# Weight buffers 64 bytes apart, a later pair of column sums, and four raw buffers in a hybrid decoder layer

## The chip, the core and the metric

The kernel runs on one core of one Trainium2 chip. The metric is device time in microseconds of one execution. TensorE multiplies, ScalarE (ACT) and VectorE (DVE) prepare operands and do the element-wise work, GpSimd (POOL) does a few powers and issues some stores, SyncE (SP) issues the loads.

## The reference, cut to what matters

One layer, 256 tokens, width 2048, all in float32:

```
h     = RMSNorm(x)
proj  = h @ W_in        # 2048 x 8192: h_conv, b, c, z_conv, q, k, v, z_attn, 1024 columns each
conv  = b * causal_depthwise_conv_w3(c * h_conv)
attn  = attention(QKnorm(q), QKnorm(k), v)       # 8 heads of 128, causal, one block of 256
y     = concat[RMSNorm(conv) * silu(z_conv), RMSNorm(attn) * silu(z_attn)]
out   = x + y @ W_out   # 2048 x 2048
```

## The kernel before

**Precision.** Every float32 weight and activation is split into a high and a low part of type fp32r, and a product is made as high times high, high times low and low times high. The weights arrive as `raw`; ACT copies the high part into `wh` (L465) and DVE subtracts it into `wl` (L466).

**Pieces.** The work is a list of 160 pieces of 512 KB of weights (L427 to L432), in this order:

- 48 pieces of the token projections q, k, v ("A"): the weight tile is the moving operand, 512 columns, and a 128 x 128 slice of the input `xs` is stationary. Three matmuls (L106 to L108) for each k-tile and each half of the tokens, so 12 matmuls in a piece.
- 80 pieces of the channel projections ("B", `by_chan`): here the weight slice is stationary and the input moves. There are 20 units of four pieces: the four groups of z_attn first, then h, c, b and z_conv for each of four channel groups. For each of four k-tiles and two 128-channel blocks of a piece there is a pair: L473 moves 512 columns (high and low input) past `wh`, L474 moves 256 columns (high input) past `wl`. Eight pairs in a piece, 640 in all.
- 32 pieces of the output projection ("Y"), again three matmuls of 512 columns.

**Buffers.** `raw`, `wh` and `wl` have five buffers each (L52), 4096 bytes a partition. The constants in front are padded (L64, L314), and in the built program every `wh`, `wl` and `xs` slice that TensorE reads begins at a multiple of 512 bytes. The constant `ones` begins 64 bytes behind such a multiple of 128.

**Order.** The order is written out by hand. At piece j the program issues the load of piece j + 6 and the split of piece j + 3, then the matmuls of piece j, then what the table `todo` holds for this slot (`at(slot, f)`). A load waits on SP until DVE has read the buffer's former content; the queue of SP is in order, so the loads behind it wait too.

**Sums over channels.** The two output norms need a sum of squares over channels. `add_squares` adds up squares on ACT and DVE; `token_sums(slot, key, f)` then, at `slot`, splits the sum into `row_h` and `row_l` (ACT L129, DVE L130), two slots later multiplies both by `ones` on TensorE (L136, L137: 256 columns each), and one slot later takes the diagonal on DVE (L144) and the root on POOL (L111). For the attention ("a") the slot is `A_DONE + 4` = 70: the two matmuls stand behind piece 72, the 25th of the 80 channel pieces. For the convolution ("c") they stand behind the first output piece. What the sums are needed for, `gather` (L485), begins with the end of the first output unit.

Of the kernel before, what the change touches and what calls it, by code (L numbers as in the profile page):

```python
# [10 lines left out]
F32 = mybir.dt.float32  # L11
FR = mybir.dt.float32r
# [5 lines left out]
P = 128  # L18
# [3 lines left out]
KT = DM // P  # L22
DG = 1024
CW = 512
# [17 lines left out]
LEAD = 3  # L42
LOADS = LEAD + 3
SINGLE = 4
NWARM = 8


@with_exitstack
def hybrid_layer(ctx: ExitStack, tc: tile.TileContext, xT, x, w_a, w_b, w_out, par, out):
    nc = tc.nc  # L50
    cst = ctx.enter_context(tc.tile_pool(name="cst", bufs=1))
    wp = ctx.enter_context(tc.tile_pool(name="wp", bufs=LEAD + 2))  # L52
# [7 lines left out]
    def aux():  # L60
        return ps.tile([P, CW], F32, name="aux", bufs=4)
# [12 lines left out]
    a = aux()  # L74
    for i in range(NWARM):
        nc.tensor.matmul(a, warm[:, :P], warm, start=i == 0, stop=i == NWARM - 1)
    spark = cst.tile([P, 1], F32, name="spark")
# [17 lines left out]
    def at(slot, f, *args):  # L95
        todo.setdefault(slot, []).append((f, args))
# [19 lines left out]
    def add_squares(key, src):  # L116

        sq = tp.tile([P, CW], F32, name="sq", bufs=2)
        nc.scalar.activation(sq, src, AF.Square)
        if key not in sums:  # L120
            s = sums[key] = cst.tile([P, SEQ], F32, name="sums_" + key)
            nc.vector.tensor_add(s, sq[:, :SEQ], sq[:, SEQ:])
        else:
            for i in range(2):
                nc.vector.tensor_add(sums[key], sums[key], sq[:, i * SEQ:(i + 1) * SEQ])

    def split_rows(src):
        hi, lo = (tp.tile([P, SEQ], FR, name=n, bufs=1) for n in ("row_h", "row_l"))
        nc.scalar.activation(hi, src, AF.Copy)  # L129
        nc.vector.tensor_tensor(lo, src, hi.bitcast(F32), op=OP.subtract)  # L130
        return hi, lo

    def partition_sums(hi, lo):

        a = aux()
        nc.tensor.matmul(a[:, :SEQ], ones, hi, start=True, stop=False)  # L136
        nc.tensor.matmul(a[:, :SEQ], ones, lo, start=False, stop=True)  # L137
        return a

    def by_token(dst, a):  # L140

        for t in range(NT):
            d = tp.tile([P, P], F32, name="diag", bufs=2)
            nc.vector.tensor_tensor_reduce(out=d, in0=a[:, t * P:(t + 1) * P], in1=ident, scale=1.0, scalar=0.0,  # L144
                                           op0=OP.mult, op1=OP.add, accum_out=dst[:, t:t + 1])

    def token_sums(slot, key, f):

        def summed(a):
            ms = tp.tile([P, NT], F32, name="ms_t", bufs=2)  # L150
            by_token(ms, a)
            f(ms)

        at(slot, lambda: at(slot + 2, lambda hl=split_rows(sums[key]): at(slot + 3, summed, partition_sums(*hl))))
# [4 lines left out]
    def load_xT(k, n):  # L159
        if k % 2 == 0:  # L160
            x_raw[k // 2] = t2k((P, 2, SEQ))
        nc.sync.dma_start(x_raw[k // 2][:, k % 2:k % 2 + n], xT[:, k:k + n])  # L162
        if k == 0:
            nc.sync.dma_start(prm, par)

    def split_x(k):
        src, g = x_raw[k // 2][:, k % 2], prm[:, G_IN + k:G_IN + k + 1]
        nc.scalar.activation(xs[:, k, 0], src, AF.Copy, scale=g)  # L168
        nc.vector.scalar_tensor_tensor(xs[:, k, 1], src, g, xs[:, k, 0].bitcast(F32), op0=OP.mult, op1=OP.subtract)
# [259 lines left out]
    pieces = []  # L429
    for kind, n, w, kts in units:  # L430
        pk, cols = (4, GW) if kind == "B" else (2, CW)
        pieces += [(kind, n, w[:, k:k + pk], k, k + pk == kts, pk, cols) for k in range(0, kts, pk)]  # L432
    raws, ws = {}, {}

    def load(j):
        if j >= len(pieces):
            return
        _, _, src, _, _, pk, cols = pieces[j]
        raw = raws[j] = wp.tile([P, pk, cols], F32, name="raw")
        if j < SINGLE:  # L440
            for i in range(2):
                nc.sync.dma_start(raw[:, i:i + 1], src[:, i:i + 1])  # L442
                load_xT(2 * j + i, 1)
            return
        if j < KT // 2:
            load_xT(2 * j, 2)
        nc.sync.dma_start(raw, src)

    def split(j):
        if j >= len(pieces):  # L450
            return
        raw = raws.pop(j)
        wh = wp.tile(list(raw.shape), FR, name="wh")
        wl = wp.tile(list(raw.shape), FR, name="wl")
        ws[j] = (wh, wl)
        if j < SINGLE:
            for i in range(2):
                nc.scalar.activation(wh[:, i], raw[:, i], AF.Copy)
                nc.vector.tensor_tensor(wl[:, i], raw[:, i], wh[:, i].bitcast(F32), op=OP.subtract)
                split_x(2 * j + i)  # L460
            return
        if j < KT // 2:
            for i in range(2):
                split_x(2 * j + i)
        nc.scalar.activation(wh, raw, AF.Copy)  # L465
        nc.vector.tensor_tensor(wl, raw, wh.bitcast(F32), op=OP.subtract)  # L466
# [34 lines left out]
    A_DONE = max(ends["A", len(A_ORDER) - 1] + 18, ends["B", NG - 1] + 3)  # L501
    for g in range(NG):
        at(ends["A", len(A_ORDER) - 1] + 12 + 2 * g, lambda g=g: add_squares("a", oT[:, g * GPT:(g + 1) * GPT]))
    token_sums(A_DONE + 4, "a", a_rms)
    e = ends["B", len(B_ORDER) - 2]
    token_sums(e + 3, "c", c_rms)
    at(e + 7, c_rms2)

    for j in range(LOADS):
        load(j)  # L510
    for j in range(LEAD):
        split(j)
    acc = None
    for j, (kind, n, _, k, last, pk, _) in enumerate(pieces):
        load(j + LOADS)
        split(j + LEAD)
        if k == 0:
            acc = ps.tile([P, 2, CW], F32, name="acc", bufs=2)
# [14 lines left out]
        else:  # L533
            n, k0 = n
# [62 lines left out]
```

## Time and profile before

| what | value |
|---|---|
| median of three runs | 472.22 us (471.61 to 472.26) |
| profiled execution | 470.43 us |
| its span, first to last instruction | 468.7 us |
| PE busy | 462.6 us, 99% |
| DVE busy / ACT busy / POOL busy | 303.9 / 242.6 / 20.1 us |
| DMA moved | 90.63 MB, mean 193 GB/s |
| granted TensorE clock | 0.999 of full speed |

How to read it: PE is busy almost from end to end, so the span is the sum of the times from the start of one matmul to the start of the next. Matmuls overlap in a pipeline: the duration that the profile gives for one is longer than the time to the next one's start, here by about 0.16 us for each. So rates are best read from the first and the last start of a group and its count, and the durations then tell by their differences which matmuls of a stretch come sooner or later.

### The profile page before, as it was taken

The page shows a single profiled execution, that of the slowest core. Times are in us where ns is not written, and L with a number is a line of the kernel's source. Part 1 is how long each engine was busy: PE and PEld are TensorE (multiplying, and loading weights), DVE is VectorE, ACT ScalarE, POOL GpSimd, SP SyncE. Part 2 cuts the span into 40 slices and gives each one's busy share as a digit, 9 for nine tenths or more (in the row PEclk, how much of TensorE's full clock was granted, in tenths as well). Part 3 has the DMA queues.
Part 4 walks back from the last instruction along what each step waited for, and adds up shares of the span by engine and source line. Part 5 has one row for each costly group of instructions (what it writes and reads, how often), then busy time and mean ns, then how long its engine had stood idle before and what let it go on. Part 6 is the DMA issues. An engine that isn't in the chain of part 4 may idle for free.

```text
span 468.7 us, 6428 instructions
## 1 busy us (share of the span) xinstructions
PE 462.6 (99%) x2416; PEld 394.6 (84%) x2416; DVE 303.9 (65%) x440; ACT 242.6 (52%) x337; POOL 20.1 (4%) x23
## 2 busy tenths in 40 slices
PE   8999999999999999999999999999999999999996
PEld 5788888888888888888888888888888888888885
DVE  5988767567475666678866675666666676566541
ACT  6975546465536667656545544455544553343320
POOL 1002200002020000000100000000000010000100
PEclk9999999999999999999999999999999999999999
DMA  8987664645665555555565556656655778766611
GB/s 256 392 258 244 206 211 140 191 136 170 180 196 162 181 172 153 166 187 179 185 206 184 188 180 190 202 185 187 199 191 175 219 238 259 246 187 201 219 67 47
DMA packets 27583, 90.63 MB, mean 193 GB/s; under 512 B 3232, under 2 KB 4512, under 8 KB 27552
## 3 DMA queue, kind: packets, MB, share of 16 engines
q1 hardware_dynamic: 27072, 88.65, 59.9%
q0 software_dynamic: 480, 1.57, 1.0%
q8 instruction: 19, 0.31, 0.3%
q14 instruction: 12, 0.10, 0.1%
HBM read 88.11 MB, written 2.10 MB: 192 GB/s over the span
## 4 chain that ended last, share of the span: by engine, by line
PE 95%; DMA 2%; SPq 1%; DVE 0%; ACT 0%; issue 0%
PE acc L473 31%; PE acc L474 16%; PE acc L107 14%; PE acc L108 14%; PE acc L106 14%; PE aux L107 1%; PE aux L106 1%; PE aux L108 1%; DMA raw<-in_w_a_dram 1%; DMA t2k<-in_xT_dram 1%; PE aux L223 1%; PE aux L283 1%; SPq L442 0%; PE aux L252 0%; PE aux L299 0%; SPq L162 0%
## 5 line engine op out<-in xcount | busy, mean ns | idle before, releaser
L466 DVE TENSOR_TENSOR wl<-raw,wh 128x1024 fp32r<-128x1024 f32 x156 | 190.3, 1223 | 99.5 <-ACT wh L465 99.1
L473 PE MATMUL acc<-xs,wh 128*128 128x512 f32 x640 | 223.4, 393 | 0.0
L465 ACT ACTIVATE wh<-raw 128x1024 fp32r<-128x1024 f32 x156 | 164.6, 1057 | 111.4 <-PE acc L108 59.5
L474 PE MATMUL acc<-xs,wl 128*128 128x256 f32 x640 | 179.1, 280 | 0.0
L473 PEld LDWEIGHTS acc<-xs,wh 128*128 128x128 f32 x640 | 119.9, 187 | 26.9
L474 PEld LDWEIGHTS acc<-xs,wl 128*128 128x128 f32 x640 | 120.9, 189 | 0.0
L106 PE MATMUL acc<-wh,xs 128*128 128x512 f32 x192 | 76.3, 397 | 0.4 <-ACT xs L168 0.4
L107 PE MATMUL acc<-wl,xs 128*128 128x512 f32 x192 | 75.1, 391 | 0.4 <-DVE wl L466 0.4
L108 PE MATMUL acc<-wh,xs 128*128 128x512 f32 x192 | 75.1, 391 | 0.0
L107 PE MATMUL acc<-wl,yh 128*128 128x512 f32 x112 | 43.6, 389 | 0.0
L108 PE MATMUL acc<-wh,yl 128*128 128x512 f32 x112 | 43.6, 389 | 0.0
L106 PE MATMUL acc<-wh,yh 128*128 128x512 f32 x112 | 43.6, 389 | 0.0
L106 PEld LDWEIGHTS acc<-wh,xs 128*128 128x128 f32 x192 | 36.3, 189 | 8.3 <-ACT xs L168 1.3
L107 PEld LDWEIGHTS acc<-wl,xs 128*128 128x128 f32 x192 | 36.4, 189 | 7.8 <-DVE wl L466 0.8
L108 PEld LDWEIGHTS acc<-wh,xs 128*128 128x128 f32 x192 | 36.2, 188 | 7.7
L338 ACT ACTIVATE t2k<-acc 128x512 f32<-128x512 f32 x20 | 11.9, 596 | 28.5 <-PE acc L474 28.5
L339 DVE TENSOR_TENSOR t2k<-acc,t2k 128x512 f32<-128x512 f32 x20 | 13.8, 691 | 18.1 <-ACT t2k L338 18.1
L106 PEld LDWEIGHTS acc<-wh,yh 128*128 128x128 f32 x112 | 21.0, 188 | 4.4
L108 PEld LDWEIGHTS acc<-wh,yl 128*128 128x128 f32 x112 | 21.0, 188 | 4.3
L107 PEld LDWEIGHTS acc<-wl,yh 128*128 128x128 f32 x112 | 21.0, 188 | 4.3
L308 ACT ACTIVATE yh<-t2k,prm 128x256 fp32r<-128x256 f32 x16 | 7.3, 503 | 16.6 <-DVE t2k L374 16.6
L111 POOL TENSOR_TENSOR r<-ms,neg_half 128x8 f32<-128x8 f32 x4 | 10.1, 2525 | 78.6 <-DVE ms L210 78.6
(117 smaller groups left out, 289.3 us busy)
## 6 DMA issues: line engine op xcount, KB each, us to landing
raw<-in_w_b_dram SPq DMA_DIRECT2D x80, 512.0 KB, 4.6
raw<-in_w_a_dram SPq DMA_DIRECT2D x44, 512.0 KB, 3.9
raw<-in_w_out_dram SPq DMA_DIRECT2D x32, 512.0 KB, 3.8
raw<-in_w_a_dram SPq DMA_DIRECT2D x8, 256.0 KB, 4.1
t2k<-in_x_dram SPq DMA_DIRECT2D x8, 256.0 KB, 4.8
out_dram<-t2k POOLq DMA_DIRECT2D x6, 256.0 KB, 3.4
t2k<-in_xT_dram SPq DMA_DIRECT2D x8, 128.0 KB, 4.1
t2k<-in_xT_dram SPq DMA_DIRECT2D x4, 256.0 KB, 5.6
```

What stands on the lines that cost most here:

```text
L106: nc.tensor.matmul(acc, sh, mh, start=first, stop=False)
L107: nc.tensor.matmul(acc, sh, ml, start=False, stop=False)
L108: nc.tensor.matmul(acc, sl, mh, start=False, stop=last)
L111: nc.gpsimd.tensor_tensor(dst, ms, neg_half[:, :ms.shape[-1]], op=OP.pow)
L223: nc.tensor.transpose(a[:, i * P:(i + 1) * P], qn[key, t][:, i], ident)
L308: nc.scalar.activation(yh[:, kt + i], src, AF.Copy, scale=g)
L338: nc.scalar.activation(d, acc[:, :, SEQ:], AF.Copy)
L339: nc.vector.tensor_add(d, acc[:, :, :SEQ], d)
L465: nc.scalar.activation(wh, raw, AF.Copy)
L466: nc.vector.tensor_tensor(wl, raw, wh.bitcast(F32), op=OP.subtract)
L473: nc.tensor.matmul(acc[:, b], wh, xs[:, k].rearrange("p s t -> p (s t)"), start=first, stop=False)
L474: nc.tensor.matmul(acc[:, b, :SEQ], wl, xs[:, k, 0], start=False, stop=last)
```

## The change

Three things are changed. The tiles `wh` and `wl` are allocated 64 floats wider (4352 bytes instead of 4096), and from piece `(n, k) >= (4, 8)` of the channel projections on (the third piece of the fifth unit, the 19th of the 80), `wh` is used from float 16 on, that is 64 bytes further; `wl` and all other pieces stay at the tile's start. To make room, `raw` has four buffers instead of five. And `token_sums` of the attention moves from slot `A_DONE + 4` to slot `e`, the last piece but four of the channel projections.

```
+SHIFT, SHIFT_FROM = 16, (4, KT // 2)
...
-        raw = raws[j] = wp.tile([P, pk, cols], F32, name="raw")
+        raw = raws[j] = wp.tile([P, pk, cols], F32, name="raw", bufs=LEAD + 1)
...
-        wh = wp.tile(list(raw.shape), FR, name="wh")
-        wl = wp.tile(list(raw.shape), FR, name="wl")
+        kind, n, _, k, _, pk, _ = pieces[j]
+
+        shift = SHIFT if kind == "B" and (n, k) >= SHIFT_FROM else 0
+        wh, wl = (wp.tile([P, 2 * CW + 64], FR, name=m)[:, o:o + 2 * CW].rearrange("p (k c) -> p k c", k=pk)
+                  for m, o in (("wh", shift), ("wl", 0)))
...
-    token_sums(A_DONE + 4, "a", a_rms)
     e = ends["B", len(B_ORDER) - 2]
+    token_sums(e, "a", a_rms)
     token_sums(e + 3, "c", c_rms)
```

In the built program the buffers of `wh` and `wl` stood 4096 bytes apart; now they stand 4352 bytes apart, so that they begin at multiples of 256 bytes and some of them no longer at multiples of 512. The lines of the changed file are five higher than before in the matmuls (L478 is L473, L479 is L474) and two higher in the sums (L138 is L136).

On TensorE, behind the 25th channel piece, before (the numbers tell the buffers apart):

```order
L474 MATMUL acc_2147<-xs_70,wl_2068 128x256
L136 MATMUL aux_2169<-row_h_2110,ones_89 128x256
L137 MATMUL aux_2169<-row_l_2111,ones_89 128x256
L473 MATMUL acc_2147<-xs_70,wh_2090 128x512
L474 MATMUL acc_2147<-xs_70,wl_2091 128x256
```

In the same place now:

```order
L478 MATMUL acc_2143<-xs_70,wh_2067 128x512
L479 MATMUL acc_2143<-xs_70,wl_2068 128x256
L478 MATMUL acc_2143<-xs_70,wh_2090 128x512
L479 MATMUL acc_2143<-xs_70,wl_2091 128x256
L478 MATMUL acc_2143<-xs_70,wh_2090 128x512
```

And two pieces ahead of the end of the channel projections, where only pairs stood before, now:

```order
L478 MATMUL acc_3419<-xs_70,wh_3367 128x512
L479 MATMUL acc_3419<-xs_70,wl_3368 128x256
L138 MATMUL aux_3466<-row_h_3409,ones_89 128x256
L139 MATMUL aux_3466<-row_l_3410,ones_89 128x256
L478 MATMUL acc_3419<-xs_70,wh_3389 128x512
L479 MATMUL acc_3419<-xs_70,wl_3390 128x256
```

The two matmuls with `ones` have moved 55 - 2 = 53 pieces back; from the last attention head to that place the stream is now pairs alone.

On SP, at the first load that is one whole piece (the fifth piece), before:

```order
L162 DMA t2k_137<-in_xT_dram 128x512 [waits DMAHW1_49]
L447 DMA raw_136<-in_w_a_dram 128x1024 [waits DMAHW2_49]
L162 DMA t2k_141<-in_xT_dram 128x512 [waits DMAHW3_49]
L447 DMA raw_140<-in_w_a_dram 128x1024 [waits DMAHW4_49,DVE_49]
L162 DMA t2k_175<-in_xT_dram 128x512 [waits DMAHW5_49]
```

and now:

```order
L164 DMA t2k_137<-in_xT_dram 128x512 [waits DMAHW1_49]
L449 DMA raw_136<-in_w_a_dram 128x1024 [waits DMAHW2_49,DVE_49]
L164 DMA t2k_141<-in_xT_dram 128x512 [waits DMAHW3_49]
L449 DMA raw_140<-in_w_a_dram 128x1024 [waits DMAHW4_49,DVE_49]
L164 DMA t2k_175<-in_xT_dram 128x512 [waits DMAHW5_49]
```

The order of the loads is the same; the fifth already waits for DVE, and each later one waits for a split that is one piece younger.

## Rows read from the trace of the kernel before

**Rows 1.** The page: busy time, and the chain that ended last by engine.

```profile
PE 462.6 (99%) x2416; PEld 394.6 (84%) x2416; DVE 303.9 (65%) x440; ACT 242.6 (52%) x337; POOL 20.1 (4%) x23
...
PE 95%; DMA 2%; SPq 1%; DVE 0%; ACT 0%; issue 0%
```

**Rows 2.** Waits of PE: waited for, us in total, times, longest us.

```profile
PE aux L76 <- DVE warm L73: 1.2, 1, 1.2
PE acc L107 <- DVE wl L466: 0.4, 1, 0.4
PE acc L106 <- ACT xs L168: 0.4, 1, 0.4
```

**Rows 3.** One line's instructions, 195 to 223 us: duration min/median/max, first and last start.

```profile
L473 PE MATMUL acc<-xs,wh x80: 395/398/403, 194.9 to 222.8; 128*128 128x512 f32 x80
L474 PE MATMUL acc<-xs,wl x80: 277/281/284, 194.8 to 222.7; 128*128 128x256 f32 x80
```

**Rows 4.** The same lines, 226 to 254 us, and L473 again from 346 to 374 us.

```profile
L473 PE MATMUL acc<-xs,wh x82: 391/391/391, 225.9 to 254.0; 128*128 128x512 f32 x82
L474 PE MATMUL acc<-xs,wl x82: 280/280/280, 225.8 to 253.8; 128*128 128x256 f32 x82
L473 PE MATMUL acc<-xs,wh x82: 391/391/391, 345.8 to 373.9; 128*128 128x512 f32 x82
```

**Rows 5.** The same two lines between attention heads, 168 to 172 us.

```profile
L473 PE MATMUL acc<-xs,wh x13: 392/392/395, 167.7 to 171.9; 128*128 128x512 f32 x13
L474 PE MATMUL acc<-xs,wl x12: 274/277/280, 167.9 to 171.8; 128*128 128x256 f32 x12
```

**Rows 6.** One of the three matmuls of token and output projections, 20-39 and 385-452 us.

```profile
L107 PE MATMUL acc<-wl,xs x28: 389/389/393, 20.0 to 38.3; 128*128 128x512 f32 x28
L107 PE MATMUL acc<-wl,yh x99: 389/389/389, 384.7 to 451.3; 128*128 128x512 f32 x99
```

**Rows 7.** Timeline of PE around the attention's column sums: start us, duration us.

```profile
223.54 0.40 PE L473 MATMUL acc<-xs,wh 128*128 128x512 f32 x1
223.78 0.28 PE L474 MATMUL acc<-xs,wl 128*128 128x256 f32 x1
223.91 0.28 PE L136 MATMUL aux<-row_h,ones 128*128 128x256 f32 x1
224.02 0.28 PE L137 MATMUL aux<-row_l,ones 128*128 128x256 f32 x1
224.14 0.40 PE L473 MATMUL acc<-xs,wh 128*128 128x512 f32 x1
...
224.49 0.39 PE L473 MATMUL acc<-xs,wh 128*128 128x512 f32 x1
```

**Rows 8.** Timelines of the start: SP's loads, DVE's splits, PE.

```profile
9.81 0.33 SPq L447 DMA_DIRECT2D raw<-in_w_a_dram  x1
...
16.49 1.23 DVE L466 TENSOR_TENSOR wl<-raw,wh 128x1024 fp32r<-128x1024 f32 x1 [0.73 <-ACT wh L465]
...
26.30 1.22 DVE L466 TENSOR_TENSOR wl<-raw,wh 128x1024 fp32r<-128x1024 f32 x1
...
17.77 0.50 PE L107 MATMUL acc<-wl,xs 128*128 128x512 f32 x1 [0.42 <-DVE wl L466]
...
28.81 0.39 PE L107 MATMUL acc<-wl,xs 128*128 128x512 f32 x1
```

**Rows 9.** DMA issues of the page (median us to landing); ACT's split of sums.

```profile
raw<-in_w_b_dram SPq DMA_DIRECT2D x80, 512.0 KB, 4.6
raw<-in_w_a_dram SPq DMA_DIRECT2D x44, 512.0 KB, 3.9
...
369.80 0.42 ACT L129 ACTIVATE row_h<-sums_c 128x256 fp32r<-128x256 f32 x1 [0.25 <-DVE sums_c L125]
```

**Rows 10.** The chain that ended last, in order of time: start us, us, what.

```profile
9.81 5.56 DMA raw<-in_w_a_dram
15.40 1.07 ACT wh L465
```

## The prediction

> **What bounds the kernel now.** I read the page first. PE is busy for 462.6 us of a span of 468.7 us, and the chain of waits that ended last is PE for 95% [rows 1]. Then the waits of PE: together 2.0 us, 1.2 us of them before the first warm-up matmul and 0.8 us at the start of the weights [rows 2]. So no other engine, buffer or load holds PE up later than the first 18 us, and the time is a sum of distances from one matmul's start to the next. A change that moves work on ACT, DVE, POOL or SP can only cost something if it makes PE wait where it does not wait today; a change in the distances counts 640 times.
>
> So the next view is the distances in the channel projections, stretch by stretch, by first start, last start and count. From 194.9 to 222.8 us 80 of L473 make 79 steps: 27.9 / 79 = 353.2 ns for a pair of L473 and L474 [rows 3]. From 225.9 to 254.0 us there are 81 steps in 28.1 us: 346.9 ns [rows 4]. The instructions, the clock and the tiles' alignment are the same. The durations tell the two stretches apart even better: in the slow one they change from matmul to matmul (395 to 403 ns and 277 to 284 ns), in the quick one all are 391 and 280 ns, and the same 391 stands 120 us later [rows 3, 4]. A third form, between attention heads, mixes 392 to 395 with 274 to 280 ns, and its sum is like the quick one's [rows 5]. So the stream of pairs falls into a beat and keeps it until something else is put into it. The attention's heads put transposes in between; the last thing that changes the beat is the pair of matmuls with `ones` at 223.91 us: before it 353.2 ns, behind it 346.9 ns to the end of the channel projections [rows 3, 4, 7]. The two forms lie 6.3 ns apart, 1.8% of a pair.
>
> The token and output projections keep one beat: 389 ns in both, and 27 steps of three matmuls in 18.3 us and 98 in 66.6 us make 226 and 227 ns for a matmul of 512 columns [rows 6].
>
> **The change part by part.**
>
> *The later column sums.* Nothing is added: two matmuls of 256 columns, 224.14 - 223.91 = 0.23 us together [rows 7], stand 53 pieces later, and the work on ACT, DVE and POOL behind them too. What needs the result begins behind the first output unit, six pieces after the matmuls, so their lateness costs 0. The new order has one new wait: `row_h` is one buffer, so ACT's split of the convolution's sums now waits until PE has read the attention's. Behind it on ACT stand the high parts of pieces that PE needs three pieces later, some 8 us at eight pairs of 347 ns a piece; the split itself takes 0.42 us [rows 9]. I take 0; if the cover were gone it would be those 0.42 us once. What the move does cost or bring is its effect on the beat: the 440 pairs of the 55 pieces behind the 25th no longer begin with a pair of matmuls that changes the beat.
>
> *Four raw buffers.* Each load now waits for a split that is one piece younger. In the steady state four pieces of 12 matmuls of 226 ns last 10.8 us; the split of one piece takes about 1.07 + 1.23 us, a load lands in 3.9 to 4.6 us [rows 8 to 10]. 10.8 - 2.3 - 4.6 leaves 3.9 us of slack. At the start it is closer. The first whole load goes out at 9.81 us, and the first buffer's halves were split long before, so it does not move; it lands 5.56 us later, and the wait of 0.42 us of PE at 17.77 us hangs on it [rows 8, 10]. The ninth piece's load must now wait for the end of the fifth's split, 16.49 + 1.23 = 17.72 us. With 3.9 to 5.6 us it lands at 21.6 to 23.3 us; DVE splits that piece at 26.30 us, and PE takes it at 28.81 us [rows 8]. So nothing becomes late, unless a landing takes 3 us more. On the other side the loads that used to share the DMA engines with the fifth go out later, which may take away up to the 0.42 us of the wait. I take -0.1 us, from -0.4 to +0.5.
>
> *The shift of 64 bytes.* From the 19th piece on 62 pieces, 496 pairs, have `wh` 64 bytes further, and `wl`, `xs` and the sums in PSUM as before. 7 x 8 = 56 of the pairs stood ahead of the matmuls with `ones` at 353.2 ns, 440 behind them at 346.9 ns. No row shows a pair with its `wh` shifted: the only stationary operand off the 128-byte grid is `ones`, and after it the beat was another one [rows 7]. So bounds. The best halves that the trace shows apart are 389 ns for 512 columns [rows 6] and 274 ns for 256 [rows 5]; against 391 + 280 that is 8 ns less, a pair of 338.9 ns: 440 x -8.0 and 56 x -14.3 ns, -4.3 us. The worst that lasted is 353.2 ns: 440 x +6.3 ns, +2.8 us. The beats that lasted are 6.3 ns apart, so the next one down is 340.6 ns, within the bound. The two operands' relative place is the only thing that the shift changes, and that the beat has forms of which one or the other is taken shows that PE's reads disturb each other. Between the known 346.9 and the possible 340.6 I take the middle, 343.7 ns: 440 x -3.2 ns = -1.4 us and 56 x -9.5 ns = -0.5 us, -1.9 us.
>
> Against this stands a rule of the Trainium skill, SBUF — State Buffer, "Who interferes with whom": TensorE has two read ports, one for the moving operand and one for loading weights, independent of each other, and never waits for anyone. By that rule an address could not matter, and the shift would be worth 0. The trace bears this out only in part: 353.2 and 346.9 ns for the same instructions show that something is waited for, but not that it depends on an address.
>
> *The wider tiles.* All buffers of `wh` and `wl` now begin at multiples of 256 bytes, not all of 512. If 256 bytes matter, the token and output projections, 48 + 32 pieces, could leave their even beat. No row shows it; between 0 and one beat's step for a tenth of their 80 x 12 = 960 matmuls, 96 x 6.3 ns = 0.6 us. I take 0.
>
> **Sum.** -0.1 - 1.9 = -2.0 us. The profiled execution took 470.43 us, 1.8 us less than the median of 472.22 us; the distances that I change are the same in both, so I take the difference off the median: 470.2 us.
>
> **Rivals.** What a measurement of this kernel can tell from no change is 0.2%, 0.9 us.
>
> *The old quick beat.* The shift does what the matmuls with `ones` did: it changes the beat once, and 346.9 ns holds from the 19th piece on. For it: in the trace two of the three forms have this sum [rows 4, 5]. Then only the 56 pairs gain, 56 x -6.3 ns = -0.35 us, and with the start 471.8 us.
>
> *The slow beat stays (slower).* The shift does nothing to the beat, or leads into the slow one, and the matmuls that ended the slow beat at 223.91 us are gone. For it: the slow beat lasted from the last head to exactly those matmuls, 80 pairs and more without change [rows 3, 7], and nothing else stands in the stream for 53 pieces. Against it: a new alignment that kept precisely the old form would be chance. Then 440 pairs have 353.2 ns: +2.8 us, 475.0 us. It is slower than before as soon as more than 150 pairs (0.9 us / 6.3 ns) behind the 25th piece keep the slow beat. By the rule of the Trainium skill just told, the shift would do nothing, and this is the case that would follow.
>
> *Raw loads late.* If a landing at the start took 3 us more, PE would wait perhaps 0.5 us once: inside the range of the others.
>
> **How the numbers follow.** A shorter beat 0.45: from 346 ns (-1.0 us) to 340.6 ns with the start's 0.4 (440 x -6.3 and 56 x -12.6 ns and -0.4 us: -3.9 us), so 468.3 to 471.2 us, likeliest 470.2 us. The old quick beat 0.28: 471.2 to 472.4 us. The slow beat 0.27: 473.2 to 475.5 us. Faster by over 0.2% (below 471.3 us): nearly all of the first and a bit of the second, 0.46. Within 0.2%: 0.28. Slower: 0.26. The range for 8 in 10 has to hold the slow case's 475.0 us and the next beat's 468.3 us: 468.2 to 475.2 us. The likeliest case's own range is 468.3 to 471.2 us.
>
> **What would show it.** In the changed kernel, the pairs' step by first start, last start and count from the 19th piece to the two matmuls with `ones`: 343.7 ns or less for this forecast, 346.9 with durations of 391 and 280 for the first rival, 353.2 with changing durations for the second. The matmuls of 512 columns in the token and output projections should keep 389 ns; if not, the wider tiles matter. The waits of PE should stay at or below 2.0 us in total; if a wait for `wl` or `wh` appears after 18 us, the raw buffers are the step that was wrong. ACT's second split of sums should wait for PE, and PE for nothing behind it.

## The result and the profile after

The changed kernel takes 468.46 us (median of 4 runs, 468.07 to 468.65) against 471.92 us (471.35 to 472.26) for the kernel before on the same chip: ratio 0.9924, 95% interval 0.9901 to 0.9947, or 3.5 us less. The prediction was 470.2 us with a range of 468.2 to 475.2 us: the sign and the place were right, the time is 1.7 us below it, and the gain is 1.5 us larger than the 2.0 us that it said. The profiled execution took 468.43 us, 2.0 us less than the one of before (470.43 us); why not 3.5 us is told below.

Busy time on the page of the changed kernel:

```profile
span 466.7 us, 6428 instructions
PE 458.7 (98%) x2416; PEld 391.2 (84%) x2416; DVE 303.8 (65%) x440; ACT 242.2 (52%) x337; POOL 20.1 (4%) x23
PEclk9999999999999999999999999999999999999999
```

PE is 3.9 us less busy than in [rows 1], with the same 2416 matmuls and the same granted clock; ACT, DVE and POOL do what they did. So what changed is how matmuls follow one another.

The two lines of a pair in the changed kernel (L478 was L473, L479 was L474), first from the 19th channel piece to the end of the channel projections, then in the stretches of [rows 4] and [rows 3]; durations min/median/max in ns, first and last start in us:

```profile
L478 PE MATMUL acc<-xs,wh x496: 389/389/389, 205.8 to 374.4; 128*128 128x512 f32 x166
...
L478 PE MATMUL acc<-xs,wh x83: 389/389/389, 225.9 to 253.8; 128*128 128x512 f32 x83
L479 PE MATMUL acc<-xs,wl x83: 276/276/276, 225.8 to 253.7; 128*128 128x256 f32 x83
...
L478 PE MATMUL acc<-xs,wh x82: 389/389/403, 194.9 to 222.8; 128*128 128x512 f32 x82
```

The first row has all 496 shifted pairs: 495 steps in 168.6 us, of which 0.23 us are the two matmuls with `ones`; 168.4 / 495 = 340.1 ns for a pair. The second and third have 82 steps in 27.9 us, 340.2 ns, against 346.9 ns in [rows 4]. All durations of a line are alike, 389 and 276 ns: a third lasting form beside 391 + 280 and 395 to 403 + 277 to 284 ns. In the last row the long durations (403) belong to the unshifted pairs ahead of 205.8 us.

Where it begins, in the timeline of PE (start us, duration us):

```profile
204.07 0.40 PE L478 MATMUL acc<-xs,wh 128*128 128x512 f32 x1
...
204.43 0.40 PE L478 MATMUL acc<-xs,wh 128*128 128x512 f32 x1
...
204.78 0.40 PE L478 MATMUL acc<-xs,wh 128*128 128x512 f32 x1
...
205.13 0.40 PE L478 MATMUL acc<-xs,wh 128*128 128x512 f32 x1
...
205.49 0.40 PE L478 MATMUL acc<-xs,wh 128*128 128x512 f32 x1
...
205.84 0.39 PE L478 MATMUL acc<-xs,wh 128*128 128x512 f32 x1
206.07 0.28 PE L479 MATMUL acc<-xs,wl 128*128 128x256 f32 x1
206.18 0.39 PE L478 MATMUL acc<-xs,wh 128*128 128x512 f32 x1
...
368.70 0.39 PE L478 MATMUL acc<-xs,wh 128*128 128x512 f32 x1
...
369.04 0.28 PE L138 MATMUL aux<-row_h,ones 128*128 128x256 f32 x1
...
369.27 0.39 PE L478 MATMUL acc<-xs,wh 128*128 128x512 f32 x1
```

The last five unshifted pairs (from 204.07 to 205.84) take 0.36, 0.35, 0.35, 0.36 and 0.35 us: the slow beat repeats every three pairs, one long and two short. The first shifted pair (205.84 to 206.18) takes 0.34 us. The change comes with the first shifted matmul and not a pair later. At 369.04 us the matmuls with `ones` go through and nothing changes. In the new beat the step is 0.23 us behind a matmul of 512 columns and 0.11 us behind one of 256: the pace of the token projections, where a matmul of 512 columns takes 226 to 227 ns [rows 6].

The waits of PE in the changed kernel (us in total, times, longest us), and the token projections:

```profile
PE acc L108 <- ACT xs L170: 1.9, 2, 1.1
PE aux L78 <- DVE warm L75: 1.2, 1, 1.2
PE acc L109 <- DVE wl L471: 0.8, 1, 0.8
...
19.48 0.50 PE L109 MATMUL acc<-wl,xs 128*128 128x512 f32 x1 [0.76 <-DVE wl L471]
...
L109 PE MATMUL acc<-wl,xs x28: 389/389/397, 20.3 to 38.7; 128*128 128x512 f32 x28
```

The waits make 3.9 us, 1.9 us more than [rows 2], all in the first 20 us. So the profiled execution of after started worse: its channel projections begin at 149.5 us, against 147.8 us before. 2.0 = 3.7 in the pairs less 1.7 at the start. The token projections keep their 389 ns [rows 6]; the tiles that no longer begin at multiples of 512 bytes cost nothing.

The start of the changed kernel: SP's load of the fifth piece, DVE's split of the second half of the first piece, and the time to landing of the input load (`t2k`) that left at 5.4 us; last that same input load in the chain of the kernel before (start us, us):

```profile
11.34 0.36 SPq L449 DMA_DIRECT2D raw<-in_w_a_dram  x1
...
6.36 0.69 DVE L464 TENSOR_TENSOR wl<-raw,wh 128x512 fp32r<-128x512 f32 x1 [0.24 <-ACT wh L463]
...
DMA to landing us min/median/max: 5.8/5.8/5.8
...
5.44 4.35 DMA t2k<-in_xT_dram
```

The load of the fifth piece goes out at 11.34 us instead of 9.81 us [rows 8]. It waits for the landing of an earlier load (DMAHW2 in the order lines above), as before, and now for a split on DVE as well. The split it needs is that of the first buffer, and that ended at 6.36 + 0.69 = 7.05 us. The earlier load is the input load of 5.44 us: it landed 4.35 us later before, at 9.79 us, and 5.8 us later now, at 11.2 us, and each time the fifth piece's load left just behind it. So the load is late because landings at the start came later. The chain of the changed kernel puts the wait down to a split on DVE that ended at 11.3 us, but that is the second buffer's, which this load does not need.

### The profile page after: what moved, and what is told of

Its sections match the earlier page's. It is cut to its first block, busy times and chain, and to the rows that moved or that the text cites. A ratio compares the mean times of both kernels' runs of the same rounds, so it can differ in the third digit from the quotient of the medians.

```text
span 466.7 us, 6428 instructions
## 1 busy us (share of the span) xinstructions
PE 458.7 (98%) x2416; PEld 391.2 (84%) x2416; DVE 303.8 (65%) x440; ACT 242.2 (52%) x337; POOL 20.1 (4%) x23
## 4 chain that ended last, share of the span: by engine, by line
PE 95%; DMA 2%; SPq 1%; DVE 0%; ACT 0%; issue 0%; DVEq 0%
PE acc L478 31%; PE acc L479 16%; PE acc L109 14%; PE acc L110 14%; PE acc L108 14%; DMA raw<-in_w_a_dram 2%; PE aux L109 1%; PE aux L108 1%; PE aux L110 1%; PE aux L225 1%; PE aux L285 1%; PE aux L254 0%; PE aux L301 0%; SPq L164 0%; SPq L444 0%; DVE wl L471 0%
## 5 line engine op out<-in xcount | busy, mean ns | idle before, releaser
L478 PE MATMUL acc<-xs,wh 128*128 128x512 f32 x640 | 219.8, 391 | 0.0
L479 PE MATMUL acc<-xs,wl 128*128 128x256 f32 x640 | 177.1, 277 | 0.0
L478 PEld LDWEIGHTS acc<-xs,wh 128*128 128x128 f32 x640 | 120.2, 188 | 25.6
L479 PEld LDWEIGHTS acc<-xs,wl 128*128 128x128 f32 x640 | 120.2, 188 | 0.0
L340 ACT ACTIVATE t2k<-acc 128x512 f32<-128x512 f32 x20 | 11.9, 595 | 27.9 <-PE acc L479 27.9
```

The costliest lines, as they stand in the source:

```text
L340: nc.scalar.activation(d, acc[:, :, SEQ:], AF.Copy)
L478: nc.tensor.matmul(acc[:, b], wh, xs[:, k].rearrange("p s t -> p (s t)"), start=first, stop=False)
L479: nc.tensor.matmul(acc[:, b, :SEQ], wl, xs[:, k, 0], start=False, stop=last)
```

## The experiments

The theory after this profile: the 64 bytes alone put the stream of pairs into a beat of 340 ns; neither the order of the sums nor the buffers have a part in it. The rival: the later sums leave the stream undisturbed, and the gain is theirs, or needs both. The first four kernels ran in one batch, with 471.25 us for the kernel before (17 runs). Where a kernel was run once, the text says so; the pairs' steps are always those of its profiled execution.

**Four raw buffers alone.** The kernel before with this line:

```
-        raw = raws[j] = wp.tile([P, pk, cols], F32, name="raw")
+        raw = raws[j] = wp.tile([P, pk, cols], F32, name="raw", bufs=LEAD + 1)
```

> The kernel before with four raw buffers instead of five, nothing else. Theory (the fifth raw buffer is not needed): the same time within 0.1%, 471.9 us, the pairs' steps as before (353 ns ahead of the matmuls with ones, 347 behind), no wait of PE after 20 us. Rival (the younger split holds the loads up at the start): 0.5 to 1 us more, 472.4 to 472.9 us, with a wait of PE for wl between 20 and 40 us.

471.47 us (470.58 to 472.5), ratio 1.000, interval 0.9983 to 1.0016. The first whole load went out at 10.84 us, and PE's waits were 2.1 us. Four buffers cost nothing that 0.16% can tell.

**No shift.** The changed kernel without its 64 bytes:

```
-SHIFT, SHIFT_FROM = 16, (4, KT // 2)
+SHIFT, SHIFT_FROM = 0, (4, KT // 2)
```

> The changed kernel with the shift set to 0: wider tiles, four raw buffers and the later sums remain. Theory (the 64 bytes alone make the short beat): the slow beat of 353 ns lasts from the last attention head to the late matmuls with ones, 440 pairs by 6.7 ns more than before, 474.9 us. Rival (the wider tiles or the missing matmuls with ones make the short beat): 340 ns and 468.5 us, as in the changed kernel; or 347 ns and about 471.6 us.

474.74 us, ratio 1.0073 (1.0057 to 1.0089). Its pairs in the stretch of [rows 4] and near the end:

```profile
L478 PE MATMUL acc<-xs,wh x80: 395/398/403, 225.9 to 253.8; 128*128 128x512 f32 x80
L479 PE MATMUL acc<-xs,wl x80: 277/281/284, 225.8 to 253.7; 128*128 128x256 f32 x80
...
L478 PE MATMUL acc<-xs,wh x84: 395/398/403, 344.6 to 373.9; 128*128 128x512 f32 x84
```

27.9 / 79 = 353.2 ns, with the changing durations of [rows 3], now 150 us long. Behind the late matmuls with `ones` (at 374.66 us) it goes on:

```profile
L478 PE MATMUL acc<-xs,wh x13: 395/398/403, 375.9 to 380.2; 128*128 128x512 f32 x13
```

So the two matmuls with `ones`, which ended the slow beat of the kernel before at 223.91 us [rows 7], do not end it here. This is the slower rival of the prediction, and without the shift it is what happens: the moved sums by themselves cost 440 x 6.7 ns = 2.9 us (3.5 us by the medians; 1.2 us more waiting at the start of the profiled execution, 3.2 against 2.0 us, may have a part in the rest).

**Early sums.** The changed kernel with the sums of the attention where they were before:

```
-    token_sums(e, "a", a_rms)
+    token_sums(A_DONE + 4, "a", a_rms)
```

> The changed kernel with the attention's column sums where they were before, behind the 25th channel piece. Theory (the beat of 340 ns belongs to the place of wh against xs and comes back after any disturbance): 468.5 us as in the changed kernel, 340 ns on both sides of the matmuls with ones. Rival (a beat lasts only until something is put into the stream): 347 ns behind them, 440 pairs by 6.7 ns, 471.4 us.

467.25 us (466.74 to 468.09), ratio 0.9918 (0.9906 to 0.993). On both sides of the matmuls with `ones` the pairs have 389 and 276 ns:

```profile
L478 PE MATMUL acc<-xs,wh x82: 389/389/403, 194.9 to 222.8; 128*128 128x512 f32 x82
...
L478 PE MATMUL acc<-xs,wh x84: 389/389/389, 225.8 to 254.0; 128*128 128x512 f32 x84
```

The shift alone has the whole gain. With the shift in place the order of the sums is worth nothing.

**Both weights shifted.** Is a weight slice off the grid cheaper by itself, or does its place beside the other one count?

```
-                  for m, o in (("wh", shift), ("wl", 0)))
+                  for m, o in (("wh", shift), ("wl", shift)))
```

> The changed kernel with wl shifted by 64 bytes as well as wh, from the same piece on. Theory A (what counts is how the stationary operand that is being loaded lies against the moving one; a load 64 bytes off costs 6.7 ns less): L473's step falls too, a pair takes 333.3 ns, 496 pairs by 6.7 ns less than in the changed kernel, 465.2 us. Theory B (what counts is how wh and wl lie against each other): they lie as before again, 347 or 353 ns, 471.6 to 474.9 us.

474.06 us, ratio 1.0062 (1.005 to 1.0074), and a beat that is even and slow:

```profile
L478 PE MATMUL acc<-xs,wh x80: 397/397/398, 225.8 to 253.7; 128*128 128x512 f32 x80
L479 PE MATMUL acc<-xs,wl x80: 281/281/281, 226.1 to 254.0; 128*128 128x256 f32 x80
```

27.9 / 79 = 353.2 ns. A shifted load is not cheaper by itself; with both shifted alike, from the same piece on, the gain is gone.

**The low weights alone.** If only the distance between the two counts, shifting the other one must do as well.

```
-                  for m, o in (("wh", shift), ("wl", 0)))
+                  for m, o in (("wh", 0), ("wl", shift)))
```

> The changed kernel with wl shifted by 64 bytes instead of wh, from the same piece on. Theory (what counts is that wh and wl lie 64 bytes apart, whichever is further): 340 ns for a pair, 468.5 us. Rival (what counts is where wh alone lies against xs, which L474 moves while wh is loaded): no short beat, 347 to 353 ns, 471.6 to 474.9 us.

471.22 us in a single run. The pairs have 391 to 396 and 278 to 281 ns; the first row goes to 372 us:

```profile
L478 PE MATMUL acc<-xs,wh x422: 391/392/396, 225.8 to 371.9; 128*128 128x512 f32 x141
L479 PE MATMUL acc<-xs,wl x81: 278/278/281, 226.0 to 253.7; 128*128 128x256 f32 x81
```

146.1 / 421 = 347.0 ns, the length of the old quick beat, and here without the early matmuls with `ones`. The distance alone is not the answer: entered at the same piece, it matters which of the two is shifted.

**Other shifts.** The first with `SHIFT` = 32 floats (128 bytes), the second with 8 (32 bytes):

```
-SHIFT, SHIFT_FROM = 16, (4, KT // 2)
+SHIFT, SHIFT_FROM = 32, (4, KT // 2)
```

> The changed kernel with a shift of 128 bytes instead of 64. Theory (the places repeat every 128 bytes, so that 128 is like 0): 353 ns, like the kernel with the shift at 0, 474.7 us. Rival (any distance between the two tiles will do): 340 ns, 468.5 us.

> The changed kernel with a shift of 32 bytes instead of 64. Theory (the memory is read in steps of 64 bytes and a half step leaves both operands in the same one): not the even 340 ns, between 343 and 353 ns, 470 to 475 us. Rival (any distance will do): 340 ns, 468.5 us.

One run each: 474.84 us at 128 bytes and 472.78 us at 32. The first row is from 128 bytes, the second from 32:

```profile
L478 PE MATMUL acc<-xs,wh x416: 392/395/401, 225.6 to 371.7; 128*128 128x512 f32 x139
```

```profile
L478 PE MATMUL acc<-xs,wh x417: 393/395/401, 225.7 to 371.8; 128*128 128x512 f32 x139
```

415 and 416 steps in 146.1 us each, 352.0 and 351.2 ns, with mixed durations. Of the three shifts tried from this piece on, only 64 bytes gives the quick beat; the rival, any distance, fell. A shift of 128 bytes is not like none (395 to 403 ns above), and that the memory is read in steps of 64 bytes no run shows. (PE waits 4.1 us at the start of the execution of 474.84 us, against 2.0 us in [rows 2].)

These four kernels were tried with one place of entry, the 19th piece. They show that at the same entry, behind the same stream, the address decides the beat; the next kernels show that the entry decides it too, so none of the four shows what its addresses could give from another piece on.

**Shifted from the start.** If 64 bytes mean 340 ns wherever they stand, the first 18 pieces must gain too.

```
-SHIFT, SHIFT_FROM = 16, (4, KT // 2)
+SHIFT, SHIFT_FROM = 16, (0, 0)
```

> The changed kernel with the shift from the first channel piece on instead of the 19th. Theory (340 ns sets in wherever wh lies 64 bytes off, between the attention heads too): the first 18 pieces lose the steps of 353 and 347 ns, 10 x 8 x 13.3 + 8 x 8 x 6.7 ns = 1.5 us less than the changed kernel, 0.989 of the kernel before. Rival (between the heads the disturbances rule, or the beat falls into a worse form there): no gain or up to 0.5 us more than the changed kernel.

473.66 us, ratio 1.0034 (1.0017 to 1.005): slower than before. Its pairs between the heads, behind them, and shortly ahead of and behind the matmuls with `ones` at 374.5 us:

```profile
L478 PE MATMUL acc<-xs,wh x14: 389/389/390, 165.6 to 171.0; 128*128 128x512 f32 x14
...
L478 PE MATMUL acc<-xs,wh x80: 395/396/396, 225.8 to 253.7; 128*128 128x512 f32 x80
L479 PE MATMUL acc<-xs,wl x80: 279/280/283, 226.0 to 253.9; 128*128 128x256 f32 x80
...
L478 PE MATMUL acc<-xs,wh x83: 395/396/396, 344.9 to 373.8; 128*128 128x512 f32 x83
...
L478 PE MATMUL acc<-xs,wh x13: 389/389/389, 375.8 to 379.9; 128*128 128x512 f32 x13
```

The theory that an address has one beat fell here. At the same 64 bytes the pairs go at 340 ns between the heads, at 27.9 / 79 = 353.2 ns from the last head on, and at 340 ns again behind the matmuls with `ones`. The shifted stream has a quick and a slow form, both lasting; which it takes must hang on what stands ahead of its first pair. That is tested next.

**The place of entry.** So the shift should also fail or succeed by the piece from which it holds. One run each, from the 16th and from the 17th piece on:

```
-SHIFT, SHIFT_FROM = 16, (4, KT // 2)
+SHIFT, SHIFT_FROM = 16, (3, 12)
```

> The changed kernel with the shift from the 16th channel piece on, three pieces earlier. The slow beat ahead of the shift repeats after three pairs, a piece has eight, so every third piece begins at the same place of the beat: the 16th like the 19th. Theory (which beat follows is decided by the place in the old beat at which the shift sets in): again 340 ns, from the 16th piece on; 3 x 8 x 13.3 ns = 0.3 us less than the changed kernel, 468.2 us. Rival (it is a matter of chance, or of the time since the last head): a slow beat of 353 ns to the end, 475 us.

```
-SHIFT, SHIFT_FROM = 16, (4, KT // 2)
+SHIFT, SHIFT_FROM = 16, (4, 0)
```

> The changed kernel with the shift from the 17th channel piece on, at another place of the three-pair beat than the 16th and the 19th. Theory (the place of the old beat decides): another outcome is possible here, 353 ns and 475 us, and if it is 340 ns, the steps right after the shift differ from those of the changed kernel. Rival (a shift after the last head always leads to 340 ns, only one that is there before the heads does not): 340 ns, 468.3 us.

467.42 us from the 16th and 474.1 us from the 17th piece: 6.7 us apart, though only eight pairs have another address. The entry from the 16th, in PE's timeline (the shift begins at 196.69 us):

```profile
195.98 0.40 PE L478 MATMUL acc<-xs,wh 128*128 128x512 f32 x1
...
196.34 0.40 PE L478 MATMUL acc<-xs,wh 128*128 128x512 f32 x1
...
196.69 0.39 PE L478 MATMUL acc<-xs,wh 128*128 128x512 f32 x1
...
197.03 0.39 PE L478 MATMUL acc<-xs,wh 128*128 128x512 f32 x1
```

and from the 17th (at 199.46 us), where behind it the slow form lasts to the matmuls with `ones`:

```profile
199.09 0.40 PE L478 MATMUL acc<-xs,wh 128*128 128x512 f32 x1
...
199.46 0.40 PE L478 MATMUL acc<-xs,wh 128*128 128x512 f32 x1
...
199.81 0.40 PE L478 MATMUL acc<-xs,wh 128*128 128x512 f32 x1
...
L478 PE MATMUL acc<-xs,wh x83: 395/395/396, 344.7 to 373.7; 128*128 128x512 f32 x83
```

The last two pairs ahead of the shift last 0.36 and 0.35 us in the first kernel, and the last one 0.37 us in the second. The slow beat of the unshifted pairs repeats every three pairs (the timeline from 204.07 us above), and with eight pairs a piece each piece ends at another place of the three. The changed kernel enters 32 pairs behind the last head, the kernel from the 16th piece 8 pairs behind it: both leave a remainder of two by three, and both come in behind a long and a short pair. The kernel from the 17th enters after 16 pairs, a remainder of one, behind the long pair. That fits the three cases seen, and in the last kernel below a fourth; entry at the third remainder (the 18th piece) was not tried.

**From the start, with early sums.** Do the matmuls with `ones` lead out of the slow form, as they seemed to in [rows 7]? The edits of the two kernels "shifted from the start" and "early sums" together.

> The shift from the first channel piece on, and the attention's column sums at their old place, behind the 25th piece. With the late sums the shift from the start ended in 353 ns from the last head to the matmuls with ones and 340 ns behind them. Theory (the two matmuls with ones lead out of the slow form into 340 ns wherever they stand): 353 ns for 11 pieces, 340 ns for 55; against the changed kernel 0.9 us less for the first 14 pieces and 0.75 us more for pieces 19 to 25, so 468.3 us, 0.992 of the kernel before. Rival (the outcome of the late ones was chance): 347 or 353 ns behind the matmuls too, 471 to 474 us.

467.82 us, ratio 0.9921 (0.9903 to 0.9938). The timeline at the matmuls with `ones` (start us, duration us):

```profile
222.47 0.40 PE L478 MATMUL acc<-xs,wh 128*128 128x512 f32 x1
...
222.82 0.40 PE L478 MATMUL acc<-xs,wh 128*128 128x512 f32 x1
...
223.18 0.28 PE L138 MATMUL aux<-row_h,ones 128*128 128x256 f32 x1
...
223.41 0.39 PE L478 MATMUL acc<-xs,wh 128*128 128x512 f32 x1
...
223.75 0.39 PE L478 MATMUL acc<-xs,wh 128*128 128x512 f32 x1
```

Pairs of 0.35 and 0.36 us ahead of them, 0.34 us behind. Two short matmuls turn the shifted stream's slow form into the quick one. They did so in all three kernels that had that form (from the start, from the 17th piece, and here), but "wherever they stand" is not shown: that form repeats every two pairs (0.35 and 0.36 us in turn), so with eight pairs a piece they always stood at the same place of it. The unshifted slow beat they ended in the kernel before, behind a long pair, and not in the one without the shift, behind a short one (374.31 to 374.66 us). That fits the place rule again, with one case each.

**All but one piece.** The theory then points to a better kernel: shifted between the heads too, unshifted in the 15th piece, in which the last head ends, so that the stream comes to the 16th as it does in the kernel from the 16th on.

```
-        shift = SHIFT if kind == "B" and (n, k) >= SHIFT_FROM else 0
+        shift = SHIFT if kind == "B" and (n, k) != (3, KT // 2) else 0
```

> The changed kernel, but the high weights are shifted in all channel pieces except the 15th, the one in which the last attention head's transposes end. Theory (the place of entry decides the form): the pairs between the heads, pieces 1 to 14, run at 340.0 ns as in the kernel shifted from the start; the unshifted 15th piece brings the stream to the same place in its rhythm as when only the 16th and later are shifted, and from the 16th on the pairs run at 340.0 ns to the end of the channel projections. Against the kernel shifted from the 16th piece that is about 110 pairs x 6.7 ns, some 0.7 to 0.9 us less: about 466.7 us, ratio to the kernel before 0.988 to 0.991. Rival (what matters is how the stream leaves the shifted pieces, or that some earlier piece was shifted at all): from the 16th piece on 353.3 ns until the matmuls with ones at about 374 us, and about 473.7 us, as in the kernel shifted from the start.

466.39 us (465.51 to 468.56), ratio 0.9902 (0.9882 to 0.9921): the quickest kernel of the study, 4.8 us below the kernel before. Its pairs between the heads (where [rows 5] have 392 to 395 ns), and from the 16th piece on:

```profile
L478 PE MATMUL acc<-xs,wh x13: 389/389/389, 154.8 to 158.9; 128*128 128x512 f32 x13
...
L478 PE MATMUL acc<-xs,wh x84: 389/389/389, 194.8 to 223.0; 128*128 128x512 f32 x84
```

28.2 / 83 = 339.8 ns. Its channel projections begin at 147.8 us and its 16th piece at 194.8 us, 47.0 us; in the kernel from the 16th piece on those are 148.8 and 196.7 us, 47.9 us. So 0.9 us more is gained up to there, the upper end of what the theory had. Against the changed kernel it was not run in one batch; by their ratios the intervals (0.9882 to 0.9921 and 0.9901 to 0.9947) still touch.

## Why the prediction was right, point by point

- **What bounds the kernel.** Right. Each difference of more than some 2 us between the profiled executions above is one of the pairs' beat, and PE waits for nothing behind the first 20 us of the changed kernel.
- **The shift.** The path was right: the place of one weight tile changes the pairs' beat, and the stream takes one of several lasting beats. The size was off. The step that failed is "Between the known 346.9 and the possible 340.6 I take the middle, 343.7 ns". The stream did not settle between two beats, it went a whole step down, to 340.0 ns. The term was -1.9 us; with 340.0 ns it is 440 x -6.7 ns and 56 x -13.3 ns, -3.7 us. The same step, "the next one down is 340.6 ns", was in the text as a bound and was the value. [rows 6] gave it too: 226.5 ns for 512 columns and half of that for 256 make 339.8 ns, an estimate of a pair that loses nothing. Two sentences of this part say more than is shown. That the beat has forms doesn't show that PE's reads disturb each other; the runs show that addresses and the stream ahead matter, not through what. And the place of `wh` against `wl` is not the only thing that the shift changes: it also moves `wh` against `xs`.
- **What was luck.** The prediction has no word on where the shift begins. Had it begun two pieces earlier, at the 17th, the same idea would have given 474.1 us, its slower rival. To that extent it was luck that it came out faster.
- **The later sums.** That their lateness costs nothing else held: ACT's second split, at 369.4 us, keeps nobody waiting on PE. That they matter by their effect on the beat held as well, though for this kernel only as a danger: without the shift they cost 2.9 us (440 x 6.7 ns), with it nothing. But that the early ones end a slow beat, as [rows 7] has it, holds only for their place there: in the kernel without the shift the late ones did not.
- **Four raw buffers.** Taken at -0.1 us, from -0.4 to +0.5; alone they measured 1.000 (0.9983 to 1.0016). The reason given for the first load, "the first buffer's halves were split long before", held: they were split by 7.05 us. "So it does not move" did not: it left 1.5 us later, behind an input load that landed later. In the profiled executions of all thirteen kernels with four buffers it left within 0.14 us of that landing (9.84 to 11.21 us), and the split had ended by 7.2 us. The prediction's sign for the raw buffers, a wait for `wl` behind 18 us, did appear (0.76 us, up to 19.48 us), but it goes back to that landing and not to a buffer. Of the 1.9 us of waiting more, 1.5 are for `xs`, which needs no raw buffer (0.4 us before, 1.9 us after), 0.4 us are for `wl`. Why the landings came later, no run tells; the last of the later kernels with four buffers started its channel projections at 147.8 us, as the kernel before. The medians bear no such loss: 3.5 us less against 3.7 us in the pairs.
- **The wider tiles.** Right, 0: 389 ns in the token projections.
- **The rivals.** The old quick beat did not come; its length is what the low weights alone give (347.0 ns). The slow beat was a real danger: it is what the same kernel does without the shift (474.74 us against the 475.0 us worked out), and what it does with the shift when that begins with the 17th or with the first channel piece. "A new alignment that kept precisely the old form would be chance" was the wrong reason against it: the new alignment has a slow form of its own, with durations of 395 to 396 and 279 to 283 ns, and as long a pair. The kernel is quick because its shift begins where it does. (The "more than 150 pairs" of that rival are 0.9 us / 6.3 ns = 143; nothing hangs on it.)
- **The rule weighed against it** (the Trainium skill, SBUF — State Buffer, "Who interferes with whom": two independent read ports, and PE waits for nobody). By it, as the prediction took it, an address could not matter. The trace does not agree: 64 bytes in the place of one weight tile move a pair from 353.2 to 340.2 ns (without and with the shift, behind the same stream), with instructions, shapes and clock alike. The measurement decides; whether the two ports meet it does not tell.

What stays open is what inside TensorE makes the beat. The runs show that, entered at the same piece, it depends on how far and which of `wh` and `wl` is shifted, and that with the same addresses it depends on the stream ahead; they don't show which accesses meet, if any do. Moving `xs` against both, and the other shifts from another piece on, would tell more; neither was tried.

## What to carry to other kernels

Where one engine is busy from end to end, read its distances from start to start by stretches. The durations tell forms apart, but even ones are not yet quick ones: 397 and 281 ns, all alike, stood for 353.2 ns. Whether there is something to gain shows against the same engine's best pace elsewhere in the trace, here 226.5 ns for 512 columns. When a beat has several forms, forecast one of the forms that the trace shows or that best pace, and not the middle, and try the place where a change begins as well as the change: here one piece more or less without the shift decided over 6.7 us. Check a layout tuned in this way again after any reorder of the matmuls ahead of it.

## What the hardware showed unexpectedly

- A pair of a 512-column and a 256-column fp32r matmul with its two weight loads lasts 340, 347 or 353 ns at the full granted clock (0.998 to 1.0 in these runs); the steps of 6.7 ns are 16 cycles at the level of 2.4 GHz. Each of these forms held for hundreds of pairs, and so did 351 and 352 ns at shifts of 32 and 128 bytes.
- The same instructions at the same addresses last 340 or 353 ns, by what ran before them. Two matmuls of 256 columns (0.23 us) turned the slow form of the shifted stream into the quick one in three kernels of three; of the unshifted stream's slow form they ended it in one kernel and not in another.
- Entered at the 19th piece, a shift of `wh` by 64 bytes gave 340 ns, by 32 or 128 bytes 351 and 352 ns, of `wl` by 64 bytes 347 ns, and of both by 64 bytes 353 ns.
